# A seven-product (Strassen–Winograd) projection: four output sums made inside PSUM instead of on VectorE

## The chip, the cores and the metric

The kernel runs on 1 core of one Trainium2 chip. The metric is device time in microseconds (us). Three runs of the kernel before gave 979.81, 979.97 and 980.25 us; their median, 979.97 us, is the time to which everything is compared.

## The reference

One layer of an encoder, on x of 512 tokens by 2048 columns, in float32. A combined input projection gives q, k, v and a gate for two groups of 16 heads; group A runs dilated sliding-window attention, group B a two-dimensional neighbourhood attention; the gated outputs go through one output projection and a layer norm.

```python
h = jnp.einsum('bsd,de->bse', x, w_in[layer])
qa, ka, va, ga, qb, kb, vb, gb = jnp.split(h, splits, axis=-1)
ya = _dilated_attention(heads(qa), heads(ka), heads(va), t5_bias)
yb = _neighbourhood_attention(heads(qb), heads(kb), heads(vb), na_rpb[layer])
ya = merge(ya) * jax.nn.silu(ga.astype(jnp.float32))
yb = merge(yb) * jax.nn.silu(gb.astype(jnp.float32))
y = jnp.concatenate([ya, yb], axis=-1).astype(x.dtype)
out = jnp.einsum('bse,ed->bsd', y, w_out[layer])
x = _layer_norm(DEEPNORM_ALPHA * x + out, ln_gain[layer], ln_bias[layer])
```

The change touches only how qa, ka, va, qb, kb and vb are computed, each a product of x (512 by 2048) with a weight block of 2048 by 1024.

## The kernel before, in words

**Precision.** A float32 operand is split into a high part and a low part (`split`, L86): ScalarE (ACT) copies it rounded to the high part, VectorE (DVE) subtracts to get the low part. Each product then takes three matmuls: high by high, high by low, low by high.

**Stages.** From 0 to about 71 us a plain block (L259) loads and splits x and computes six gate columns. From there to about 547 us run six seven-product blocks (`strassen_block`, L341), in the order k, q, v of group A and k, q, v of group B. Then comes attention, mixed with the remaining gate columns and the first half of the output projection as filler matmuls, to about 900 us, and last the rest of the output projection and the norm.

**A seven-product block.** x and the weights are cut into two by two quarters; seven products of sums of quarters replace eight plain ones. The four weight quarters are called q0, q1, q2 and q3, each in four tiles `braw` of 128x1024 (512 KB), loaded by `load` (L345) through SyncE's DMA queue (SP). Quarters are changed in place: `add` (L358) makes q0+=q1, q1+=q3, q0+=q3 and q0+=q2 as the products go on. The products run in the order 1, 5, 7, 6, 3, 2, 4. Each has four steps u (called jobs below, 28 per block); a job is 24 matmuls of 256 columns (k and q) or 12 of 512 columns (v), on two PSUM banks `acc` (t = 0 and 1).

**Who runs ahead.** `run_blocks` (L452) writes the order of TensorE (PE), DVE and ACT by hand. In iteration n DVE adds for job n+3 (`add`), ACT makes the high part of job n+2 (`high`, L362), then come the functions listed in `behind` for iteration n (loads, sums and stores), then DVE makes the low part of job n+2 (`low`, L367), and PE runs job n. So ACT and DVE are some two jobs ahead of PE. The order of SP's queue is not written by hand: the framework's scheduler sets it, and the queue is worked through in that order.

**PSUM.** Eight banks: four in pool `pacc`, two in `pss` (scores use it later) and two in `pst` (transposes use it later). Product 1 takes the two of `pss`, 5 and 7 those of `pacc`, 6 those of `pst`, 3 again `pss`, 2 and 4 again `pacc`.

**Sums.** After product 6, `combine_` (L431) makes on DVE, for each t, w = r1 - p6 (r1 is a copy of p1 made by ACT, L429), u3 = w - p7, c22 = p5 - u3 and w = p5 - w. `plus` (L438) then adds p3 to w, p2 to r1 and p4 to u3. That is 7 operations for each t, 84 over the six blocks. Each result is stored (`store_kq` L229, `store_v` L217): ACT copies it to `kst` or `vst`, DVE subtracts for the low part, SP writes both to `k_d`, `q_d` or `v_d` in DRAM.

**Shared memory slots.** The four sums r1, w, u3, c22 of a block lie in slots t0 to t3. After the last block the attention's first tiles take them over: `load_kq` (L534) puts k of the first pair of heads into t0 and q into t1 (two DMAs of 256 KB, L544), `load_v` (L547) puts its v into t2. `scores(0)` (L607) is the first work of attention that PE does; it stands in PE's order 49 gate matmuls (L516) behind the last block. SP's loads of weights for these, `wraw` (L495), are in the same queue.

**A side job.** In the first block, behind product 5, `rows` (L146) makes two small matmuls L149 for the bias table, on banks of `pss`.

Of the kernel before, what the change touches and what calls it, by code (L numbers as in the profile page):

```python
# [10 lines left out]
ALU = mybir.AluOpType  # L11
# [59 lines left out]
def hybrid_layer(tc, xT, xn, w_in, w_early, w_gate, w_out, t5x, brow, rpb, cmask, eye, gain, lbias, out):  # L71
    nc = tc.nc
    from contextlib import ExitStack
    with ExitStack() as ctx:
# [4 lines left out]
        pacc = ctx.enter_context(tc.tile_pool(name="pacc", bufs=4, space=bass.MemoryType.PSUM))  # L79
        pss = ctx.enter_context(tc.tile_pool(name="pss", bufs=2, space=bass.MemoryType.PSUM))  # L80
        pst = ctx.enter_context(tc.tile_pool(name="pst", bufs=2, space=bass.MemoryType.PSUM))
# [24 lines left out]
        def bank(pool, name):  # L106
            tag = {id(pacc): "acc", id(pss): "sc", id(pst): "pt"}[id(pool)]
            return pool.tile([128, 512], F32, name=name, tag=tag)
# [29 lines left out]
        def prep_a():  # L138
            nc.gpsimd.dma_start(ident, eye)
            bt = ring_b.next("bias")  # L140
            t5 = bt[0:33, 1024:1040]
            nc.gpsimd.dma_start(bt[0:33, :ROW], brow)
            nc.gpsimd.dma_start(t5, t5x)
            row = ring_b.next("bias")

            def rows():  # L146
                for i in range(2):
                    ps = bank(pss, "sc")
                    nc.tensor.matmul(ps[0:16], t5, bt[0:33, 512 * i:512 * i + 512], start=True, stop=True)  # L149
                    nc.scalar.activation(row[0:16, 512 * i:512 * i + 512], ps[0:16], AF.Copy)  # L150
                for c in range(16):
                    nc.gpsimd.dma_start(rows_d[:, c], row[0:16, :ROW])
            return rows
# [94 lines left out]
        def store(kind, g, ch, half, t, src):  # L248
            if kind == "v":
                store_v(g, ch, half, t, src)  # L250
            else:
                store_kq(kind, g, ch, half, t, src)
# [69 lines left out]
        def combine(k, xr, sums):  # L322

            a11, a21, a12, a22 = (xr[:, s, HALF * i:HALF * i + HALF] for s in range(2) for i in range(2))
            c = sums.next("sums")[:, :1024].rearrange("p (n q) -> p n q", n=4)
            nc.vector.tensor_tensor(c[:, 0], a21, a22, ALU.subtract)
            nc.vector.tensor_tensor(c[:, 1], a11, c[:, 0], ALU.subtract)
            nc.vector.tensor_tensor(c[:, 2], a12, c[:, 1], ALU.subtract)
            nc.vector.tensor_tensor(c[:, 3], a21, a11, ALU.subtract)
            split(c[:, 0], A5[k][:, 0], A5[k][:, 1])  # L330
            split(c[:, 1], A6[k][:, 0], A6[k][:, 1])
            split(c[:, 2], A3[k][:, 0], A3[k][:, 1])
            split(c[:, 3], X[k][:, 0, HALF:], X[k][:, 1, HALF:])
# [7 lines left out]
        def strassen_block(src, kind, g, hooks):  # L341

            base = len(jobs)

            def load(q, tags):  # L345
                def run():
                    for u in range(4):
                        raw = slot(tags[u], F32, "braw")
                        nc.sync.dma_start(raw, src[4 * q + u])
                        raws[q].append(raw)  # L350
                return run

            raws = {q: [] for q in range(4)}

            def product(i, pool, q, other=None):
                accs = []

                def add(u):  # L358
                    if other is not None:
                        nc.vector.tensor_tensor(raws[q][u], raws[q][u], raws[other][u], ALU.add)  # L360

                def high(u):  # L362
                    h = halves.next("wh", F32R)
                    nc.scalar.activation(h, raws[q][u], AF.Copy)  # L364
                    return h

                def low(u, h):  # L367
                    l = halves.next("wl", F32R)
                    nc.vector.tensor_tensor(l, raws[q][u], f(h), ALU.subtract)  # L369
                    return h, l  # L370

                def run(u, h, l):
                    if u == 0:
                        accs.extend(bank(pool, "acc") for _ in range(2))
                    for t in range(2):
                        for kk in range(2):
                            k = 2 * u + kk
                            ah, al = operand(i, k)
                            if kind == "k":
                                ah, al = (m.rearrange("p (b r c) -> p r b c", r=4, b=4) for m in (ah, al))  # L380
                            if kind == "v":
                                c = slice(512 * kk, 512 * kk + 512)
                                q = slice(128 * t, 128 * t + 128)
                                nc.tensor.matmul(accs[t], ah[:, q], h[:, c], start=k == 0, stop=False)  # L384
                                nc.tensor.matmul(accs[t], al[:, q], h[:, c], start=False, stop=False)  # L385
                                nc.tensor.matmul(accs[t], ah[:, q], l[:, c], start=False, stop=k == 7)  # L386
                                continue
                            for n in range(2):
                                c = slice(512 * kk + 256 * t + 128 * n, 512 * kk + 256 * t + 128 * n + 128)
                                o = accs[t][:, HALF * n:HALF * n + HALF]  # L390
                                nc.tensor.matmul(o, h[:, c], ah, start=k == 0 and n == 0, stop=False)  # L391
                                nc.tensor.matmul(o, h[:, c], al, start=False, stop=False)  # L392
                                nc.tensor.matmul(o, l[:, c], ah, start=False, stop=k == 7 and n == 1)  # L393
                    if u == 3:
                        next(hooks, lambda: None)()

                jobs.extend((lambda u=u: add(u), lambda u=u: high(u), lambda h, u=u: low(u, h),
                             lambda h, l, u=u: run(u, h, l)) for u in range(4))
                return accs

            def at(product_, u, fn):

                behind.setdefault(base + 4 * product_ + u, []).append(fn)

            def sub(o, x, y):
                nc.vector.tensor_tensor(o, x, y, ALU.subtract)

            made = {}

            def pair(name):  # L410
                if name not in made:
                    t = temps.next(name)
                    made[name] = [t[:, :512], t[:, 512:]]
                return made[name]

            p1 = product(1, pss, 0)
            p5 = product(5, pacc, 0, 1)
            p7 = product(7, pacc, 1, 3)
            p6 = product(6, pst, 0, 3)
            p3 = product(3, pss, 3)  # L420
            p2 = product(2, pacc, 2)
            p4 = product(4, pacc, 0, 2)
            tags = list(sets)
            for q, ahead, i in ((0, 10, 0), (1, 4, 1), (3, 2, 2)):
                behind.setdefault(base - ahead if base else -4, []).append(load(q, tags[i]))
            at(2, 2, load(2, tags[1]))

            def keep(t):
                nc.scalar.activation(pair("r1")[t], p1[t], AF.Copy)  # L429

            def combine_(t):  # L431
                r1, w, u3, c22 = (pair(n)[t] for n in ("r1", "w", "u3", "c22"))
                sub(w, r1, p6[t])
                sub(u3, w, p7[t])
                sub(c22, p5[t], u3)
                sub(w, p5[t], w)

            def plus(name, p, t):  # L438
                o = pair(name)[t]
                nc.vector.tensor_tensor(o, p[t], o, ALU.add)  # L440

            for t in range(2):
                at(1, t, lambda t=t: keep(t))
                at(4, t, lambda t=t: combine_(t))
                for n, name, p in ((5, "w", p3), (6, "r1", p2), (7, "u3", p4)):
                    at(n, t, lambda t=t, name=name, p=p: plus(name, p, t))
            for t in range(2):
                for n, name, ch, half in ((4, "c22", 1, 1), (5, "w", 1, 0), (6, "r1", 0, 0), (7, "u3", 0, 1)):
                    at(n, t + 1, lambda t=t, name=name, ch=ch, half=half: store(kind, g, ch, half, t, pair(name)[t]))
            sets[0], sets[2] = sets[2], sets[0]  # L450

        def run_blocks():  # L452
# [307 lines left out]
        with tc.manual_schedule(engines=engines):  # L760
# [6 lines left out]
            for n in range(136):  # L767
                b, i = n % 4, n // 8
# [177 lines left out]
        for dc in (2, 3):  # L946
            for u in range(4, 8):
                raw = out_ring.next("wraw")
                nc.sync.dma_start(raw[:, :1024], w_out[8 * dc + u])
                i = 2 * (u - 4)  # L950
# [80 lines left out]
```

## Time and profile before

| what | value |
|---|---|
| median of three runs | 979.97 us (979.81 to 980.25) |
| span of the profiled execution | 978.4 us |
| PE, matmul busy | 968.1 us |
| PE, weight loads busy (PEld) | 855.0 us |
| DVE busy | 756.8 us |
| ACT busy | 486.6 us |
| SP's queue, share of 16 DMA engines' span | 56.6% |
| granted TensorE clock, mean | 0.996 |

The profile gives the span of one profiled execution, from its first to its last instruction, and no time of its own beside it; the median of the runs is 1.57 us above that span. A matmul's row gives its start and its modelled length; since matmuls are pipelined, the pace of PE is read from the distance of the starts. A row of the DMA-issuing queue (SPq) tells when a transfer was issued, not when it landed.

### The profile page before, as it was taken

How to read it: one execution, taken by the hardware profiler on the slowest of the kernel's cores; microseconds unless marked ns; L12 is line 12 of the kernel's file. 1: busy time of each engine (PE TensorE's matmuls, PEld its weight loads, DVE VectorE, ACT ScalarE, POOL GpSimd, SP SyncE). 2: the span in 40 equal slices, each digit the busy share in tenths (PEclk: the TensorE clock that was granted, in tenths of full speed). 3: DMA queues.
4: the chain of work that ended last, by engine and by line, in shares of the span. 5: the costliest groups of instructions: out<-in, count | busy, mean ns of one | idle time of the engine just before them, and what ended most of it. 6: DMA issues, size and time to landing. Idle time of an engine off the chain costs nothing.

```text
span 978.4 us, 16019 instructions
## 1 busy us (share of the span) xinstructions
PE 968.1 (99%) x5851; PEld 855.0 (87%) x5851; DVE 756.8 (77%) x1152; ACT 486.6 (50%) x839; POOL 179.0 (18%) x327
## 2 busy tenths in 40 slices
PE   9999999999999999999999999999999999999996
PEld 6889999999888999999888888888888888888885
DVE  7947788788988977878889567676676767777877
ACT  7534344344444434434454366666666666762300
POOL 1000665664553400000000001010010000100021
PEclk9999999999999999999999999999999999999998
DMA  9731688599569638428634967777777788768322
GB/s 341 289 120 55 164 276 270 177 255 273 178 188 302 185 95 277 116 87 232 165 120 113 343 185 217 194 232 234 188 222 224 197 238 205 209 223 293 90 75 97
DMA packets 118014, 194.29 MB, mean 199 GB/s; under 512 B 48351, under 2 KB 67551, under 8 KB 117936
## 3 DMA queue, kind: packets, MB, share of 16 engines
q1 hardware_dynamic: 105104, 169.15, 56.6%
q0 software_dynamic: 12256, 23.47, 8.7%
q8 instruction: 46, 0.75, 0.3%
q10 hardware_dynamic: 576, 0.66, 0.2%
q14 instruction: 32, 0.26, 0.1%
HBM read 148.68 MB, written 44.50 MB: 197 GB/s over the span
## 4 chain that ended last, share of the span: by engine, by line
PE 96%; DVE 1%; ACT 1%; DMA 1%; issue 0%; SPq 0%; DVEq 0%; ACTq 0%
PE acc L710 15%; PE acc L516 11%; PE acc L391 11%; PE acc L393 11%; PE acc L392 11%; PE acc L384 5%; PE acc L386 5%; PE acc L385 5%; PE pv L662 4%; PE pt L640 4%; PE acc L270 2%; PE sc L621 2%; PE acc L272 2%; PE acc L271 2%; PE sc L620 2%; PE sc L710 1%
## 5 line engine op out<-in xcount | busy, mean ns | idle before, releaser
L364 ACT ACTIVATE wh<-braw 128x1024 fp32r<-128x1024 f32 x168 | 178.3, 1061 | 254.9 <-PE acc L392 130.9
L369 DVE TENSOR_TENSOR wl<-braw,wh 128x1024 fp32r<-128x1024 f32 x168 | 206.4, 1229 | 65.6 <-ACT wh L364 65.3
L391 PE MATMUL acc<-xk,wh 128*128 128x256 f32 x512 | 144.5, 282 | 0.0
L393 PE MATMUL acc<-xk,wl 128*128 128x256 f32 x512 | 144.4, 282 | 0.0
L392 PE MATMUL acc<-xk,wh 128*128 128x256 f32 x512 | 144.4, 282 | 0.0
L360 DVE TENSOR_TENSOR braw<-braw 128x1024 f32<-128x1024 f32 x96 | 118.8, 1237 | 0.0
L710 PE MATMUL acc<-wh,yk 128*128 128x512 f32 x320 | 108.4, 402 | 0.0
L392 PE MATMUL acc<-op,wh 128*128 128x256 f32 x384 | 108.4, 282 | 0.0
L391 PE MATMUL acc<-op,wh 128*128 128x256 f32 x384 | 108.3, 282 | 0.0
L393 PE MATMUL acc<-op,wl 128*128 128x256 f32 x384 | 108.3, 282 | 0.0
L646 DVE TENSOR_TENSOR tl<-pt,th 128x256 fp32r<-128x256 f32 (+1 forms) x128 | 71.1, 555 | 48.0 <-ACT th L645 46.8
L391 PEld LDWEIGHTS acc<-xk,wh 128*128 128x128 f32 x512 | 97.2, 190 | 0.9 <-ACT bias L150 0.9
L392 PEld LDWEIGHTS acc<-xk,wh 128*128 128x128 f32 x512 | 97.2, 190 | 0.1
L393 PEld LDWEIGHTS acc<-xk,wl 128*128 128x128 f32 x512 | 97.2, 190 | 0.0
L645 ACT ACTIVATE th<-pt 128x256 fp32r<-128x256 f32 (+1 forms) x128 | 62.3, 489 | 65.0 <-PE pt L640 62.9
L516 PE MATMUL acc<-xk,wh 128*128 128x512 f32 x320 | 90.8, 402 | 0.0
L577 DVE CUSTOM_DVE_ANT_0 s<-sc,biases 128x512 f32<-128x512 f32 (+2 forms) x128 | 68.1, 532 | 17.9 <-PE sc L621 17.3
L581 ACT ACTIVATE p<-s,mn 128x512 f32<-128x512 f32 (+1 forms) x96 | 62.1, 647 | 25.6 <-DVE mn L577 25.2
L392 PEld LDWEIGHTS acc<-op,wh 128*128 128x128 f32 x384 | 72.9, 190 | 0.0
L393 PEld LDWEIGHTS acc<-op,wl 128*128 128x128 f32 x384 | 72.9, 190 | 0.0
L391 PEld LDWEIGHTS acc<-op,wh 128*128 128x128 f32 x384 | 72.9, 190 | 0.0
L710 PEld LDWEIGHTS acc<-wh,yk 128*128 128x128 f32 x320 | 58.4, 189 | 9.1 <-ACT yk L694 0.3
(183 smaller groups left out, 2026.1 us busy)
## 6 DMA issues: line engine op xcount, KB each, us to landing
braw<-in_w_in SPq DMA_DIRECT2D x96, 512.0 KB
wraw<-in_w_out SPq DMA_DIRECT2D x32, 512.0 KB
wraw<-in_w_gate SPq DMA_DIRECT2D x20, 512.0 KB
k_d<-kst SPq DMA_DIRECT2D x64, 128.0 KB
q_d<-kst SPq DMA_DIRECT2D x64, 128.0 KB
v_d<-vst SPq DMA_DIRECT2D x32, 256.0 KB
q<-q_d SPq DMA_DIRECT2D x32, 256.0 KB
k<-k_d SPq DMA_DIRECT2D x16, 512.0 KB
```

Source lines behind the costliest of these rows:

```text
L360: nc.vector.tensor_tensor(raws[q][u], raws[q][u], raws[other][u], ALU.add)
L364: nc.scalar.activation(h, raws[q][u], AF.Copy)
L369: nc.vector.tensor_tensor(l, raws[q][u], f(h), ALU.subtract)
L391: nc.tensor.matmul(o, h[:, c], ah, start=k == 0 and n == 0, stop=False)
L392: nc.tensor.matmul(o, h[:, c], al, start=False, stop=False)
L393: nc.tensor.matmul(o, l[:, c], ah, start=False, stop=k == 7 and n == 1)
L516: nc.tensor.matmul(acc, w[:, k * 128:k * 128 + 128], X[8 * u + k][:, s], start=u == 0 and n == 0 and k == 0, stop=u == 1 and n == 2 and k ...
L577: nc.vector.tensor_tensor_reduce(*flat, bias, 1.0, 3e38, ALU.add, ALU.min, mn)
L581: nc.scalar.activation(p[:, to:to + n].rearrange("p (b r c) -> p b r c", r=8, c=c), s[:, :n].rearrange(order, r=8, c=c), AF.Exp, bias=mn, ...
L645: nc.scalar.activation(th, pt[:, :nch], AF.Copy)
L646: nc.vector.tensor_tensor(tl, pt[:, :nch], f(th), ALU.subtract)
L710: nc.tensor.matmul(acc[:, part], yk[k][:, s, c], w[:, wk], start=first and kk == 0 and n == 0, stop=last and kk == 1 and n == 2)
```

## The change

Products 2, 3 and 4 no longer get banks of their own. Product 2 runs on top of product 1's banks, product 3 on product 5's and product 4 on product 7's: their matmuls have no start flag, so that PSUM adds them to what is there. For that, the order of the last three products becomes 2, 3, 4, and the operand of product 7 changes its sign (a11 - a21 instead of a21 - a11).

The sums become: w = r1 - p6; u3 = p7 + w; c22 = p5 - u3 (before products 2, 3 and 4 write on the banks); then c11 is product 1's bank itself, from which ACT and DVE store directly; c12 = p5 - w goes to r1; c21 = p7 + w goes to w. That is 5 operations for each t, 60 over six blocks. c11, c12 and c21 are stored in this order, in the iterations in which w, r1 and u3 were. In the last block, w (slot t1) is thus read last by c21, and u3 (slot t2) is done with after `combine_`.

The load of the next block's q0, into the slots that q3 leaves, is listed six iterations ahead of that block instead of ten, since q3 is used one product later. The load of q2 stays in iteration 10 of its block, and q2 is used one product earlier. The two small matmuls L149 get banks of `pst`, since those of `pss` are held longer.

```diff
             def rows():
                 for i in range(2):
-                    ps = bank(pss, "sc")
+                    ps = bank(pst, "pt")
...
-            nc.vector.tensor_tensor(c[:, 3], a21, a11, ALU.subtract)
+            nc.vector.tensor_tensor(c[:, 3], a11, a21, ALU.subtract)
...
-            def product(i, pool, q, other=None):
-                accs = []
+            def product(i, pool, q, other=None, onto=None):
+                accs = [] if onto is None else onto
+                first, skip = onto is None, onto is not None
...
-                    if u == 0:
+                    if u == 0 and first:
                         accs.extend(bank(pool, "acc") for _ in range(2))
...
-                                nc.tensor.matmul(o, h[:, c], ah, start=k == 0 and n == 0, stop=False)
+                                nc.tensor.matmul(o, h[:, c], ah, start=first and k == 0 and n == 0, stop=False, skip_group_check=skip)
...
-            p3 = product(3, pss, 3)
-            p2 = product(2, pacc, 2)
-            p4 = product(4, pacc, 0, 2)
+            product(2, None, 2, onto=p1)
+            product(3, None, 3, onto=p5)
+            product(4, None, 0, 2, onto=p7)
             tags = list(sets)
-            for q, ahead, i in ((0, 10, 0), (1, 4, 1), (3, 2, 2)):
+            for q, ahead, i in ((0, 6, 0), (1, 4, 1), (3, 2, 2)):
...
                 sub(w, r1, p6[t])
-                sub(u3, w, p7[t])
+                nc.vector.tensor_tensor(u3, p7[t], w, ALU.add)
                 sub(c22, p5[t], u3)
-                sub(w, p5[t], w)
-
-            def plus(name, p, t):
-                o = pair(name)[t]
-                nc.vector.tensor_tensor(o, p[t], o, ALU.add)
+
+            def last(name, t):
+                r1, w = pair("r1")[t], pair("w")[t]
+                if name == "c12":
+                    sub(r1, p5[t], w)
+                    return r1
+                if name == "c21":
+                    nc.vector.tensor_tensor(w, p7[t], w, ALU.add)
+                    return w
+                return p1[t] if name == "c11" else pair("c22")[t]
...
-                for n, name, p in ((5, "w", p3), (6, "r1", p2), (7, "u3", p4)):
-                    at(n, t, lambda t=t, name=name, p=p: plus(name, p, t))
             for t in range(2):
-                for n, name, ch, half in ((4, "c22", 1, 1), (5, "w", 1, 0), (6, "r1", 0, 0), (7, "u3", 0, 1)):
-                    at(n, t + 1, lambda t=t, name=name, ch=ch, half=half: store(kind, g, ch, half, t, pair(name)[t]))
+                for n, name, ch, half in ((4, "c22", 1, 1), (5, "c11", 0, 0), (6, "c12", 1, 0), (7, "c21", 0, 1)):
+                    at(n, t + 1, lambda t=t, name=name, ch=ch, half=half: store(kind, g, ch, half, t, last(name, t)))
```

**What moves, place 1: SP's queue at the end of the first block.** `braw` are the weight tiles, `k_d<-kst` the stores of this block's results (eight DMAs for c22, then four for each half of the next). Before:

```order
L319 DMA sg_d<-sg 128x512 x6
L349 DMA braw<-in_w_in 128x1024 x7
L243 DMA k_d<-kst 64x2x256 x8
L349 DMA braw<-in_w_in 128x1024 x2
L243 DMA k_d<-kst 64x2x256 x4
```

Now:

```order
L319 DMA sg_d<-sg 128x512 x6
L349 DMA braw<-in_w_in 128x1024 x4
L243 DMA k_d<-kst 64x2x256 x8
L349 DMA braw<-in_w_in 128x1024 x4
L243 DMA k_d<-kst 64x2x256 x4
```

The seven loads ahead of c22's stores were four of q2 and three of the next block's q0; now only q2's four stand there, and all four of the next q0 stand behind the stores.

**Place 2: DVE at the end of the last block.** `r` and `u` are r1 and u3, `wl<-wraw` is the low part of a gate weight of the next stage, `vst` the low part of a stored result. Before:

```order
L223 TENSOR_TENSOR vst<-r_5368,vst 128x8x64
L502 TENSOR_TENSOR wl<-wraw,wh 128x1024 x2
L440 TENSOR_TENSOR u_5586<-acc,u_5586 128x512 x2
L502 TENSOR_TENSOR wl<-wraw,wh 128x1024
L223 TENSOR_TENSOR vst<-u_5586,vst 128x8x64 x2
```

Now:

```order
L223 TENSOR_TENSOR vst<-r_5318,vst 128x8x64
L506 TENSOR_TENSOR wl<-wraw,wh 128x1024
L444 TENSOR_TENSOR w<-acc,w 128x512
L223 TENSOR_TENSOR vst<-w,vst 128x8x64
L444 TENSOR_TENSOR w<-acc,w 128x512
L506 TENSOR_TENSOR wl<-wraw,wh 128x1024
L223 TENSOR_TENSOR vst<-w,vst 128x8x64
```

The last two sums stood together and their low parts behind the third gate weight; now sum and low part alternate, and the last reader of w (slot t1) is the last of them.

**Place 3: SP's queue at the turn to attention.** `q<-q_d` x2 is the load of q for the first pair, without which `scores(0)` can't start; `v_d<-vst` are the stores of the last block. Before:

```order
L544 DMA q<-q_d 64x2x512 x2
L495 DMA wraw<-in_w_gate 128x1024 x4
L226 DMA v_d<-vst 64x4x256 x4
L542 DMA k<-k_d 128x1024
L495 DMA wraw<-in_w_gate 128x1024 x3
L604 DMA biases<-biasa_d 128x560
L226 DMA v_d<-vst 64x4x256 x4
L553 DMA vv<-v_d 128x1024
```

Now:

```order
L499 DMA wraw<-in_w_gate 128x1024
L226 DMA v_d<-vst 64x4x256 x2
L546 DMA k<-k_d 128x1024
L499 DMA wraw<-in_w_gate 128x1024
L226 DMA v_d<-vst 64x4x256 x2
L499 DMA wraw<-in_w_gate 128x1024
L608 DMA biases<-biasa_d 128x560
L226 DMA v_d<-vst 64x4x256 x2
L548 DMA q<-q_d 64x2x512 x2
```

The load of q for the first pair has gone from ahead of four gate weights to behind the last store of v; the load of `vv` has gone the other way, ahead of all stores of v.

More of the change, by code (lines that the diff above doesn't have):

```diff
@@ L383, in run @@
                                 q = slice(128 * t, 128 * t + 128)
-                                nc.tensor.matmul(accs[t], ah[:, q], h[:, c], start=k == 0, stop=False)
-                                nc.tensor.matmul(accs[t], al[:, q], h[:, c], start=False, stop=False)
-                                nc.tensor.matmul(accs[t], ah[:, q], l[:, c], start=False, stop=k == 7)
+                                nc.tensor.matmul(accs[t], ah[:, q], h[:, c], start=first and k == 0, stop=False, skip_group_check=skip)
+                                nc.tensor.matmul(accs[t], al[:, q], h[:, c], start=False, stop=False, skip_group_check=skip)
+                                nc.tensor.matmul(accs[t], ah[:, q], l[:, c], start=False, stop=k == 7, skip_group_check=skip)
                                 continue
@@ L390, in run @@
                                 o = accs[t][:, HALF * n:HALF * n + HALF]
-                                nc.tensor.matmul(o, h[:, c], ah, start=k == 0 and n == 0, stop=False)
-                                nc.tensor.matmul(o, h[:, c], al, start=False, stop=False)
-                                nc.tensor.matmul(o, l[:, c], ah, start=False, stop=k == 7 and n == 1)
+                                nc.tensor.matmul(o, h[:, c], ah, start=first and k == 0 and n == 0, stop=False, skip_group_check=skip)
+                                nc.tensor.matmul(o, h[:, c], al, start=False, stop=False, skip_group_check=skip)
+                                nc.tensor.matmul(o, l[:, c], ah, start=False, stop=k == 7 and n == 1, skip_group_check=skip)
                     if u == 3:
```

## The prediction

> **What bounds the kernel now.** I read the page first, then what PE waited for, then the stage of the six seven-product blocks alone.
>
> ```profile
> span 978.4 us, 16019 instructions
> PE 968.1 (99%) x5851; PEld 855.0 (87%) x5851; DVE 756.8 (77%) x1152; ACT 486.6 (50%) x839; POOL 179.0 (18%) x327
> PE 96%; DVE 1%; ACT 1%; DMA 1%; issue 0%; SPq 0%; DVEq 0%; ACTq 0%
> ```
>
> PE is busy for 99% of the span, and the chain of work that ended last runs through PE for 96% of it. The list of waits of PE and of its weight loads (engine and line, who ended the wait, total, times, longest):
>
> ```profile
> PE pt L909 <- DVE nms L907: 2.5, 1, 2.5
> PE sc L124 <- POOL calm L121: 1.3, 1, 1.3
> PEld acc L391 <- ACT bias L150: 0.9, 1, 0.9
> ```
>
> The two longest lie at the start (L124) and in the last norm (L909). In the six blocks there is one, 0.9 us, behind the bias table's matmuls. The stage by itself (PE, PEld, DVE, ACT, POOL busy, then clock, DMA share, GB/s):
>
> ```profile
> 92.00:540.00 448.00, 448.00 (x3161) 421.29 (x3160) 373.28 (x381) 199.98 (x224) 135.02 (x253) 1.00 0.65 193
> ```
>
> PE has no gap in 448 us, at the full granted clock; DVE is at 373.28 of 448, that is 83%, and is not waited for. So whatever the change takes from DVE here is taken from an engine that has time left, and the time moves only if PE's own work, its pace, or a wait of PE changes.
>
> **The sums.** Per block and half, 7 operations become 5, so 24 of 84 go.
>
> ```profile
> L440 DVE TENSOR_TENSOR w<-acc,w 128x512 f32<-128x512 f32 x12 | 8.2, 684 | 0.0
> L440 DVE TENSOR_TENSOR r<-acc,r 128x512 f32<-128x512 f32 x12 | 8.2, 684 | 0.0
> ```
>
> 24 operations of 684 ns are 16.4 us of DVE. They lie beside PE's work, which the list of waits shows not to wait for DVE there: worth 0. On the other side the change removes no matmul and adds none: 3360 in the six blocks before and now. That products 2 to 4 add onto a bank instead of starting one is what all but the first matmul of a product do already, at the same pace: 0. Their banks must have been read first (p1 by ACT's copy, p5 and p7 by `combine_`); those reads stand a product or more earlier in the order, 11 us at least, so no wait. The stores of c11 read PSUM instead of SBUF, on two engines with time to spare: 0. The sign of the operand: 0. The bias matmuls on banks of `pst`: these are free until product 6, one product later: 0.
>
> **The weight loads.** q2 is issued as before and used one product, four jobs, earlier; q0 of the next block is issued four jobs later, behind c22's stores (place 1). Is there room? SP's queue at the end of the first block, and ACT's first uses of the next block's q0:
>
> ```profile
> 115.50 6.87 SPq L349 DMA_DIRECT2D braw<-in_w_in  x3
> 125.29 5.31 SPq L243 DMA_DIRECT2D k_d<-kst  x8
> 130.64 3.27 SPq L349 DMA_DIRECT2D braw<-in_w_in  x2
> 147.03 1.06 ACT L364 ACTIVATE wh<-braw 128x1024 fp32r<-128x1024 f32 x1 [1.25 <-PE acc L392]
> 155.55 1.06 ACT L364 ACTIVATE wh<-braw 128x1024 fp32r<-128x1024 f32 x1 [1.81 <-DMA k_d<-kst]
> ```
>
> The first of them was issued at 115.50 and used at 147.03. Now all four start behind the stores, from about 130.6 us on, and are used at 147.03 to 155.55: the margin of the first shrinks from 31 to 16 us. For q2 the first load was issued at 90.78 (in the fence below) and now is wanted by ACT about two jobs ahead of product 2's place, 118.6 - 5.8 = 112.8 us with a product of 11.3 us: 22 us of room. What a load takes under full load is shown at the turn to attention:
>
> ```profile
> 90.78 31.59 SPq L349 DMA_DIRECT2D braw<-in_w_in  x7
> 534.29 1.78 SPq L544 DMA_DIRECT2D q<-q_d  x2
> 536.16 2.21 SPq L495 DMA_DIRECT2D wraw<-in_w_gate  x4
> 541.99 1.06 ACT L501 ACTIVATE wh<-wraw 128x1024 fp32r<-128x1024 f32 x1 [1.20 <-DMA wraw<-in_w_gate]
> 545.00:557.00 12.00, 12.00 (x54) 9.95 (x53) 4.93 (x6) 2.29 (x4) 0.00 (x0) 1.00 1.03 362
> ```
>
> ACT waited until 541.99 for a tile of the same 512 KB whose issue began at 536.16: 5.8 us from issue to use. 5.8 is well below 16 and 22, so the loads stay hidden: 0. That ACT waits for a `braw` load hardly at all now agrees (3.7 us in two waits for a load, against 187.8 us for PE to free a buffer):
>
> ```profile
>   PE acc L392: 130.9, 78
>   PE acc L385: 56.9, 37
>   DMA braw<-in_w_in: 3.7, 2
> ```
>
> **The one load that comes too late.** Slot t1 holds w. Before, w's last reader stood in the last product but one, and q of the first pair was issued at 534.29, long before `scores(0)` needs it. Now w is read last by c21 at the very end (place 2), and q stands behind the last store of v (place 3). What ends the block, and when PE wants q:
>
> ```profile
> 546.36 1.35 DVE L440 TENSOR_TENSOR u<-acc,u 128x512 f32<-128x512 f32 x2
> 547.81 1.13 ACT L222 ACTIVATE vst<-u 128x512 fp32r<-128x512 f32 x2
> 547.93 1.23 DVE L502 TENSOR_TENSOR wl<-wraw,wh 128x1024 fp32r<-128x1024 f32 x1 [0.22 <-ACT wh L501]
> 549.08 1.29 DVE L223 TENSOR_TENSOR vst<-u,vst 128x512 fp32r<-128x512 f32 x2
> 550.25 3.83 SPq L226 DMA_DIRECT2D v_d<-vst  x4
> 557.70 0.19 PEld L620 LDWEIGHTS sc<-k,q 128*128 128x128 f32 x1
> bias<-rows_d POOLq DMA_DIRECT2D x128, 35.0 KB, 3.4
> sg_d<-sgo POOLq DMA_DIRECT2D x10, 256.0 KB, 4.7
> ```
>
> By the new order DVE goes on from 546.36 with: sum 0.68, ACT's copy 0.6, low part 0.69, sum 0.68, third gate weight 1.23, low part 0.69, which ends at 550.9, about 551.0 with the handovers (before: 549.08 + 1.29 = 550.4). Then SP issues two stores, at 3.83 / 4 = 0.97 us each (0.6 where it isn't held up), and q's two DMAs, of which the second begins 1.78 / 2 = 0.89 us behind the first: 551.0 + 1.9 + 0.9 = 553.8 at the latest, 552.9 at 0.6 each. Take 553.6. From issue to landing I have three rows: 3.4 us for a 35 KB DMA of POOL, 4.7 us for POOL's 256 KB, the same size, and the 5.8 us above for 512 KB on this queue. The DMA engines are full here (share 1.03 from 545 to 557), which speaks against the low end. Landing: 552.9 + 3.4 = 556.3, 553.6 + 4.7 = 558.3, or 553.8 + 5.8 = 559.6. PE's weight load for `scores(0)` began at 557.70, and every matmul of PE queues behind it. So PE stands for 0, 0.6 or 1.9 us. I take 0.6, from the row of the same size, and keep 0 and 1.9; that PE doesn't stand at all has a quarter of the chance. In the stages behind it PE has no gap in which this would be given back.
>
> Here a rule can be weighed. The Trainium skill, "DMA: Bandwidth & Descriptors", Anatomy of one DMA, gives a fixed cost of about 2.0 us plus the bytes at 436 GB/s; by it 256 KB would take an estimated 2.6 us, q would land at about 556.2 and PE would not stand at all, which makes the sum 0.6 us smaller. The trace disagrees for this stage, with 4.7 us for the same size.
>
> **PE's pace.** The starts of k's matmuls show two paces in one block. Rows of PE, the first and last of 88 and of 59 matmuls, and the bias matmuls between the two stretches:
>
> ```profile
> 83.51 0.28 PE L393 MATMUL acc<-op,wl 128*128 128x256 f32 x1
> 93.95 0.28 PE L393 MATMUL acc<-op,wl 128*128 128x256 f32 x1
> 94.16 1.89 PE L149 MATMUL sc<-bias 33*16 33x512 f32 x4
> 139.49 0.28 PE L391 MATMUL acc<-xk,wh 128*128 128x256 f32 x1
> 146.31 0.28 PE L392 MATMUL acc<-xk,wh 128*128 128x256 f32 x1
> ```
>
> Before the bias matmuls 10.44 us / 87 = 120.0 ns from start to start; after them 6.82 / 58 = 117.6 ns, to the end of that block. A product of 96 such matmuls gains 0.23 us by the second pace, the five products left in this block 1.2 us. I don't know what sets it; it begins right behind L149. L149 stays where it is, so I keep the pace: 0. If the new bank upsets it, 1.2 us are lost; if other blocks of k or q should fall into it, each gains up to 7 x 0.23 = 1.6 us, all 23 products now at 120 ns 5.3 us.
>
> **The sum.** Of the profiled execution: 978.4 + 0.6 = 979.0; the 1.57 us by which the median lies above this span I leave as they are. So 979.97 + 0.6 = 980.6 us.
>
> **Rivals.**
> The weights come late (slower). Place 1 puts q0 behind the stores; the next q1 and q3 follow in the same queue, so some 1.5 MB move into the stretch that is fullest. If the first tile took over 16 us from issue to use, ACT's `high` and with it PE would wait, once at each of five turns of blocks: each 1 us beyond that point costs 5 us, 985 us for the first. For it: the queue is worked through in order, and at the turn to attention the DMA share is 1.03. Against: 5.8 us measured there. Chance 0.10.
> q comes later still (slower). If q's two DMAs wait behind all of the gate weights and stores, with 8 us instead of 5.8 from issue to landing, PE stands until 561.8, over 4 us: 984. The point from which it leaves "no change" is a landing at 559.7. Chance 0.10.
> PE is not full (faster). The 968.1 us busy are of modelled ends. In the row of the stage the weight loads take 421.29 of 448.00 us, 94%; if the 26.7 us left were a slackness that DVE's work causes, less DVE would free some of it, or of the pace: with all of k and q at 117.6 ns, 980.6 - 5.3 = 975.3 us. The Trainium skill, "Perfetto Trace Analysis", Identifying the Most-Contended Engine, says just that matmul busy time is no good measure of headroom and that weight-load time is. Against it here: the starts are 120.0 ns apart over 88 matmuls without one irregular step, and the waits name no DVE in this stage. Chance 0.08.
> That the change doesn't do what it says can be left out: DVE's order has 24 rows fewer.
>
> **The numbers.** No change is my forecast, 0.72. Two kernels this close can be told apart by about 0.2%, which is 1.96 us: faster means below 978.0, slower above 981.9. Faster 0.08, same 0.72, slower 0.20. The range takes in both ends of q's landing and the loss of the faster pace upward, 979.9 + 1.9 + 1.2 = 983.0, and a gain of one k or q block's pace without any wait for q downward, 980.6 - 1.6 = 979.0.
>
> **What would show it.** Right: DVE busy lower by about 16 us and the span within 2 us; in the list of waits one new row, PE or PEld at `sc<-k,q`, released by the DMA of q, of 0 to 2 us at about 558 us; no `braw` among the waits of PE. Wrong: ACT idle before its high parts for `braw` by many us at each block's start; a wait of PE for q of 3 us or more; or starts of k's and q's matmuls closer than 120 ns in blocks where they are not now.

## The result: 985.74 us, slower by half a per cent

| | before | changed |
|---|---|---|
| median of four runs | 979.89 us (979.39 to 980.25) | 985.74 us (982.07 to 986.57) |
| ratio, with 95% interval | | 1.0053 [1.0041, 1.0064] |
| profiled execution, time | | 986.57 us |
| its span | 978.4 us | 984.8 us |
| granted TensorE clock, mean | 0.996 | 0.992 |

The kernel before has one run more here than in its table above, so its median is 979.89 and not 979.97 us. The changed kernel is slower by 5.9 us. The forecast was 980.6 us in a range up to 983.0, so it was wrong: the wait that it named came, at the place that it named, but several times as long, and something came behind it that no step had foreseen.

The page of the changed kernel (span; busy time of each engine; the granted clock in 40 slices; the shares of the chain that ended last):

```profile
span 984.8 us, 15984 instructions
PE 971.0 (99%) x5851; PEld 857.8 (87%) x5851; DVE 742.0 (75%) x1128; ACT 487.7 (50%) x839; POOL 180.3 (18%) x327
PEclk9999999999999999999999899999999999999998
PE 95%; DVE 1%; ACT 1%; DMA 1%; issue 0%; SPq 0%; POOL 0%; DVEq 0%; ACTq 0%; POOLq 0%
```

DVE is down from 756.8 to 742.0 us with 24 instructions fewer, as meant, and nothing of that reached the span. One digit is new: slice 23 of 40, about 542 to 566 us, has a clock below 9. The stage of the six blocks by itself, in the same columns as before (PE, PEld, DVE, ACT, POOL, clock, DMA share, GB/s):

```profile
92.00:540.00 448.00, 448.00 (x3161) 421.31 (x3161) 357.92 (x356) 200.81 (x224) 136.23 (x253) 1.00 0.64 195
```

PE had no gap there before and has none now; 15.4 us of DVE are gone and PE's row is the same, 448.00 us and 3161 matmuls. So the loss lies behind the blocks. The list of waits shows where:

```profile
PEld sc L624 <- issue: 4.3, 1, 4.3
PE sc L624 <- DMA q<-q_d: 4.0, 1, 4.0
PEld acc L392 <- ACT bias L150: 0.9, 1, 0.9
```

The last row is the old one. The first two are one and the same new wait, seen from the weight load and from the matmul: `scores(0)` stood for q. No row of PE or PEld names a `braw`. The timeline of DVE at that place (start, duration, operation, and in brackets what was waited for), and that of SP's queue:

```profile
547.29 0.69 DVE L444 TENSOR_TENSOR w<-acc,w 128x512 f32<-128x512 f32 x1 [0.81 <-PE acc L387]
549.29 0.69 DVE L444 TENSOR_TENSOR w<-acc,w 128x512 f32<-128x512 f32 x1
551.02 0.68 DVE L223 TENSOR_TENSOR vst<-w,vst 128x512 fp32r<-128x512 f32 x1
```

```profile
552.00 0.64 SPq L608 DMA_DIRECT2D biases<-biasa_d  x1
552.74 1.24 SPq L226 DMA_DIRECT2D v_d<-vst  x2
554.03 2.10 SPq L548 DMA_DIRECT2D q<-q_d  x2
```

The first sum starts at 547.29 where the forecast had 546.36, the last low part ends at 551.70, SP is then busy with `biases` until 552.64, issues the two stores and comes to q at 554.03. What happened to q stands in the chain of waits that ended last (start, duration, what):

```profile
554.88 7.07 DMA q<-q_d
561.94 0.14 issue
562.08 0.77 PE sc L624
```

7.07 us from the second issue to the landing. And then PE, first before, then changed:

```profile
557.70 0.39 PE L516 MATMUL acc<-xk,wh 128*128 128x512 f32 x1
557.93 0.39 PE L620 MATMUL sc<-k,q 128*128 128x512 f32 x1
558.38 2.43 PE L516 MATMUL acc<-xk,wh 128*128 128x512 f32 x10
```

```profile
557.74 0.39 PE L520 MATMUL acc<-xk,wh 128*128 128x512 f32 x1
562.08 0.77 PE L624 MATMUL sc<-k,q 128*128 128x512 f32 x1 [3.95 <-DMA q<-q_d]
563.07 4.27 PE L520 MATMUL acc<-xk,wh 128*128 128x512 f32 x10
```

PE reached the same point at the same time, 557.7. `scores(0)` then starts 562.08 - 557.93 = 4.15 us late. But the span is 6.4 us longer. The last rows tell where the other 2.2 us went: the same ten matmuls take 4.27 us instead of 2.43. The windows of the changed kernel (columns as above, the clock third from the end):

```profile
555.00:560.00 5.00, 3.13 (x14) 2.25 (x12) 0.00 (x0) 0.60 (x1) 0.00 (x0) 1.00 1.04 320
560.00:562.00 2.00, 0.00 (x0) 0.00 (x0) 0.00 (x0) 0.00 (x0) 0.00 (x0) 0.54 1.01 250
562.00:564.00 2.00, 1.92 (x5) 1.56 (x6) 0.69 (x3) 0.00 (x0) 0.00 (x0) 0.50 1.04 213
564.00:566.00 2.00, 2.00 (x6) 1.58 (x5) 0.61 (x3) 1.76 (x3) 0.59 (x1) 0.50 0.40 101
566.00:568.00 2.00, 2.00 (x8) 1.57 (x7) 0.16 (x1) 0.00 (x0) 0.00 (x0) 0.76 0.34 131
568.00:570.00 2.00, 2.00 (x11) 1.58 (x10) 1.68 (x3) 0.82 (x2) 0.00 (x0) 1.00 0.00 0
```

The granted clock falls to a half while PE stands (0.54 in 560 to 562 is a half from about 560.2 on) and comes back at about 567.0 (0.76 in 566 to 568). From 562.1 to 567.0 PE works at half speed: 4.9 us in which 2.4 us of work are lost. 4.15 + 2.4 = 6.55 us, and the span is 6.4 us longer: the two terms are the loss, to 0.2 us.

### The profile page after: what moved, and what is told of

It is laid out like the page before. It is cut to its first block, busy times and chain, and to the rows that moved or that the text cites. A ratio compares the mean times of both kernels' runs of the same rounds, so it can differ in the third digit from the quotient of the medians.

```text
span 984.8 us, 15984 instructions
## 1 busy us (share of the span) xinstructions
PE 971.0 (99%) x5851; PEld 857.8 (87%) x5851; DVE 742.0 (75%) x1128; ACT 487.7 (50%) x839; POOL 180.3 (18%) x327
## 4 chain that ended last, share of the span: by engine, by line
PE 95%; DVE 1%; ACT 1%; DMA 1%; issue 0%; SPq 0%; POOL 0%; DVEq 0%; ACTq 0%; POOLq 0%
PE acc L714 14%; PE acc L392 11%; PE acc L394 11%; PE acc L393 11%; PE acc L520 10%; PE acc L386 5%; PE acc L387 5%; PE acc L385 5%; PE pv L666 4%; PE pt L644 4%; PE acc L270 2%; PE acc L271 2%; PE acc L272 2%; PE sc L625 2%; PE sc L624 2%; PE sc L714 1%
## 5 line engine op out<-in xcount | busy, mean ns | idle before, releaser
L392 PEld LDWEIGHTS acc<-xk,wh 128*128 128x128 f32 x512 | 97.2, 190 | 0.9 <-ACT bias L150 0.9
L393 PEld LDWEIGHTS acc<-xk,wh 128*128 128x128 f32 x512 | 97.2, 190 | 0.1
L520 PE MATMUL acc<-xk,wh 128*128 128x512 f32 x320 | 92.8, 409 | 0.0
L520 PEld LDWEIGHTS acc<-xk,wh 128*128 128x128 f32 x320 | 58.4, 193 | 10.1
```

Source lines behind the costliest of these rows:

```text
L392: nc.tensor.matmul(o, h[:, c], ah, start=first and k == 0 and n == 0, stop=False, skip_group_check=skip)
L393: nc.tensor.matmul(o, h[:, c], al, start=False, stop=False, skip_group_check=skip)
L520: nc.tensor.matmul(acc, w[:, k * 128:k * 128 + 128], X[8 * u + k][:, s], start=u == 0 and n == 0 and k == 0, stop=u == 1 and n == 2 and k ...
```

## The experiments

The theory to be tried: the whole loss comes from one line, the one that gives the last sum of the block to slot t1, in which q is to land; first as a stand of PE, then as a half clock that the stand brings. The rivals: the rest of the change costs something of its own, as sums that read PSUM longer, a change of PE's order or pace, or a DMA queue with more in it; or the saving on DVE is worth something that is hidden behind the loss.

Times of a run are given beside runs of the kernel before on the same chip; those had medians of 979.75 us (first four), 979.73 (e5) and 979.87 us (e6, e7).

**e1_after_swap: the changed kernel with the late sum in another slot.** u3 and w change their slots, so that the sum that is read last lies in t2, which v takes over much later, and t1 is done with after `combine_`.

```diff
-                r1, w, u3, c22 = (pair(n)[t] for n in ("r1", "w", "u3", "c22"))
+                r1, u3, w, c22 = (pair(n)[t] for n in ("r1", "u3", "w", "c22"))
```

> The changed kernel with w and u3 changing slots: u3, done with after the seven products' first sums, lies in t1, which q of the first pair takes over; w lies in t2. Nothing else differs. Theory T (all of the loss is q's late load at the turn to attention: 4.0 us that PE stands and then half the TensorE clock for 6.8 us): q is issued before the stores of v again, PE has no wait at sc<-k,q, time 979.9 us, at most 0.6 us off; DVE's 16 us less are worth nothing. Rival P (adding onto banks in PSUM, or the later weight loads, cost time in the six blocks): about 985.7 us, as the changed kernel. Rival D (lighter DVE is worth something that the loss hid): below 979.0 us.

Measured: 979.5 us (978.18 to 981.78, 11 runs), ratio 0.9999 [0.9991, 1.0008]. Its page, its timeline of SP's queue and its timeline of PE:

```profile
PE 967.2 (99%) x5851; PEld 854.8 (87%) x5851; DVE 743.1 (76%) x1128; ACT 487.7 (50%) x839; POOL 181.1 (19%) x327
```

```profile
518.01 0.63 SPq L548 DMA_DIRECT2D q<-q_d  x1
520.35 0.59 SPq L548 DMA_DIRECT2D q<-q_d  x1
```

```profile
556.93 0.39 PE L624 MATMUL sc<-k,q 128*128 128x512 f32 x1
```

q is issued some 35 us earlier, `scores(0)` has no wait, and the loss is gone. All else of the change is still there, the 24 sums fewer among it: DVE has 743.1 us. So the rest of the change costs nothing that can be measured, and it also brings nothing: 13.7 us of DVE work taken away are worth 0 here, within 0.1%, which is 0.9 us either way. Both kinds of rival fall, as far as they were to explain 5.9 us.

**e2_before_swap: the same edit in the kernel before.** None of the change's work, only the late slot.

```diff
-                r1, w, u3, c22 = (pair(n)[t] for n in ("r1", "w", "u3", "c22"))
+                r1, u3, w, c22 = (pair(n)[t] for n in ("r1", "u3", "w", "c22"))
```

> The kernel before with the same two slots exchanged, so that u3, read last at the very end of the last block, lies in t1 and q of the first pair must wait for it. Seven sums, own banks for all products. Theory T: the loss appears without any of the change's work: PE stands 3 to 5 us at sc<-k,q, granted clock halved behind it, 984 to 987 us. Rival P: no more than 980.5 us.

Measured: 982.6 us (982.58 to 984.72, 5 runs), ratio 1.0036 [1.0024, 1.0049]: slower, but by less than was expected. Its list of waits and its chain:

```profile
PEld sc L620 <- issue: 2.6, 1, 2.6
PE sc L620 <- DMA q<-q_d: 2.2, 1, 2.2
```

```profile
555.20 5.28 DMA q<-q_d
560.61 0.47 PE sc L620
```

A loss of this kind, about half as large, appears without any of the change. In the profiled execution it is the stand alone, 2.6 us, and the span grows by 2.4 us, from 978.4 to 980.8; the half clock that was expected behind it is missing there, and the mean clock stayed 0.996. q lands 5.28 us after its second issue here, 7.07 in the changed kernel.

**e3_after_busy: the changed kernel, PE kept at work while q is on its way.** 16 matmuls that nobody uses, on one bank, ahead of `scores(0)`; 16 at 0.227 us are 3.6 us.

```diff
+                if n == 0:
+                    spare = bank(pacc, "acc")
+                    for _ in range(16):
+                        nc.tensor.matmul(spare, X[0][:, 0, 0:128], X[0][:, 0], start=True, stop=True)
```

> The changed kernel with 16 matmuls of 512 columns, whose result nobody reads, ahead of scores(0): 16 x 0.227 = 3.6 us of work in the time in which PE stood. Theory T with the clock as a term of its own: PE stands only some 0.5 us, the granted clock stays at 1.0, and the time is that of before plus 4.1 = 984.0 us (983.4 to 984.6), with little spread between runs. If the halved clock costs nothing: as the changed kernel, 985.7 to 986.5 us. If PE's stand were hidden work that could be filled at a cost: 985.7 + 3.6 = 989.3 us.

Measured: 983.5 us (982.39 to 984.26, 5 runs), ratio 1.0038 [1.0026, 1.0051]. PE at that place, and the clock:

```profile
556.65 3.79 PE L787 MATMUL acc<-xk 128*128 128x512 f32 x16
560.41 0.47 PE L624 MATMUL sc<-k,q 128*128 128x512 f32 x1
560.96 2.43 PE L520 MATMUL acc<-xk,wh 128*128 128x512 f32 x10
```

```profile
560.00:562.00 2.00, 2.00 (x9) 1.40 (x9) 0.84 (x3) 0.11 (x1) 0.00 (x0) 1.00 1.05 229
```

The ten matmuls behind take 2.43 us again, at a clock of 1.00. q is issued as late as before: at 552.94, in a profiled execution in which PE gets to this place 1.1 us earlier. Useless work in place of the stand makes the kernel faster by 985.74 - 983.5 = 2.2 us. So the half clock is a term of its own. Of the 2.2 us some 0.5 are only that 3.6 us of useless work are less than a stand of 4.15, which leaves 1.7 us for the clock; the trace gave 2.4. The runs of the changed kernel scatter by more than this difference, so about 2 us is all that can be said of its size. The rest, 983.5 - 979.75 = 3.75 us, is the 3.6 us of useless work, to 0.15 us.

**e4_after_mid: the changed kernel, c21 written into u3's slot.** Another way to the same end as e1: w's last reader is then the sum itself, and not the store's two steps behind it.

```diff
-                    nc.vector.tensor_tensor(w, p7[t], w, ALU.add)
-                    return w
+                    u3 = pair("u3")[t]
+                    nc.vector.tensor_tensor(u3, p7[t], w, ALU.add)
+                    return u3
```

> The changed kernel with c21 written into u3's slot instead of w's: w (t1) is then free behind the last sum, some 1.7 us earlier on DVE, and SP's order has q ahead of the last two stores of v, the last gate weight and the biases. Theory T: q is issued at about 550 to 552 us instead of 554 to 555, PE stands 0 to 1.5 us, too short for the clock to fall: 979.9 to 981.4 us. Rival P: 985.7 us.

Measured: 979.76 us (977.94 to 980.82, 11 runs), ratio 0.9998 [0.9989, 1.0007]. q's two issues moved from 554.0 to 550.6 (the timelines of SP's queue and of PE):

```profile
550.61 1.86 SPq L549 DMA_DIRECT2D q<-q_d  x2
```

```profile
557.83 0.39 PE L625 MATMUL sc<-k,q 128*128 128x512 f32 x1
```

No wait is left. With e1, e4 and the changed kernel there are three times of q's first issue, 518.0, 550.6 and 554.0, and the loss sets in between the last two; in e7, below, an issue at 552.9 still costs 2.2 us.

**e7_q_pool: the changed kernel, q issued by POOL.** What the 7.07 us consist of was still open: q's place behind other transfers in SP's queue, or engines that are full whoever issues. Only the first pair's q is moved to the other queue.

```diff
-                nc.sync.dma_start(f(to), q_d[g][j][n // 2].rearrange("(a c) q -> c a q", a=2))
+                (nc.sync if i or n > 1 else nc.gpsimd).dma_start(f(to), q_d[g][j][n // 2].rearrange("(a c) q -> c a q", a=2))
```

> The changed kernel, with the two DMAs of the first pair's q issued by POOL instead of SP. Slot t1 is free at 551.7 us, so POOL can issue them at about 551.8 and 552.5 us, without the two stores of v ahead of them (SP issued them at 554.0 and 554.9). Theory A: the 7.0 us from the second issue to the landing were time behind SP's own queue. Then they land as POOL's 256 KB did elsewhere, 4.7 us behind the second issue, at about 557.2 us, when PE reaches scores(0) at 558.1: no wait, no half clock, 979.5 to 980.5 us. Theory B: they were the 16 DMA engines, full whatever queue is used. Then the landing is again about 7 us behind the second issue, at 559.5, and PE stands some 1.5 us, too short for the clock to halve: 981 to 982 us. In both the loss falls below half of the 5.9 us; if it stays above 4 us, the lateness of the slot is not what costs.

Measured: 982.09 us (980.38 to 983.08, 11 runs), ratio 1.0019 [1.0011, 1.0028]. Its chain of waits and its list of waits:

```profile
552.94 0.62 POOL q L548
553.56 7.29 DMA q<-q_d
561.10 0.47 PE sc L624
```

```profile
PEld sc L624 <- issue: 2.5, 1, 2.5
PE sc L624 <- DMA q<-q_d: 2.1, 1, 2.1
```

Theory B holds: on POOL's queue, where nothing else had been issued in the ten us before, q takes 7.29 us. So it is not SP's queue; what is left is that the 16 engines are full, with a DMA share of 0.87 from 554 to 556 us and of 0.98 to 1.07 from there to 562. The Trainium skill, "DMA: Bandwidth & Descriptors", Issuing engines are not separate DMA queues, says just this, that DMAs of all issuing engines end on the same 16 DMA engines and interleave there; these two numbers, 7.07 and 7.29 us, agree. The smaller loss comes from the earlier issue, without the stores ahead, and from a stand of 2.1 us behind which the clock stayed at 1.00 in the profiled execution. The issue was later than expected, 552.94 for about 551.8: all of this execution runs 0.8 us later, and the chain has the load of the first pair's k, which landed at 552.68, just ahead of it.

**e5_pace: e1 with small matmuls that might set PE's pace.** The prediction had left open why k's matmuls run at 117.6 ns behind the bias matmuls L149 and at 120.0 ns elsewhere. Two fp32 matmuls with weights of 33x16, like those (a pair shows as four records), ahead of the first product of blocks 1 (q, 512 columns), 3 (k, 512 columns) and 4 (q, 64 columns), counted from 0.

```diff
+                    if u == 0 and i == 1 and base in (28, 84, 112):
+                        w_ = 64 if base == 112 else 512
+                        for _ in range(2):
+                            spare = bank(pst, "pt")
+                            nc.tensor.matmul(spare[0:16, 0:w_], f(X[0][0:33, 0, 0:16]), f(X[0][0:33, 0, 0:w_]), start=True, stop=True)
```

> The changed kernel with the slots exchanged, plus two float32 matmuls of 33 rows and 16 columns of weights, like the bias table's L149, whose result nobody reads, ahead of product 1 of the second block (q, 512 columns moved), the fourth (k, 512) and the fifth (q, 64). Question: is it such a matmul that brings k's matmuls from 120.0 to 117.6 ns from start to start? If it is, the k block behind it runs at 117.6 ns (1.6 us less over seven products), the two q blocks too if it isn't tied to k's access pattern, and the time is 979.5 + 3 x 1.9 at most for the added work - 1.6 to 4.8 us. If it is not: all three blocks at 120.0 ns, time 979.5 plus about 4.2 us for the added matmuls.

Measured: 982.85 us (982.57 to 983.1, 6 runs), ratio 1.0033 [1.002, 1.0046]. The matmuls cost about 2 us for each pair of 512 columns (1.89 us in the row at the end of this text), more than the pace gives back. The pace itself is read from how many matmuls start in 50 us of a block; first k of group B (320 to 370), then q (400 to 450), in the changed kernel and in e5:

```profile
320.00:370.00 50.00, 50.00 (x419) 50.00 (x418) 39.52 (x38) 20.03 (x21) 5.85 (x13) 1.00 0.36 101
400.00:450.00 50.00, 50.00 (x419) 50.00 (x418) 38.96 (x38) 20.15 (x22) 0.00 (x0) 1.00 0.35 94
```

```profile
320.00:370.00 50.00, 50.00 (x428) 50.00 (x427) 40.41 (x39) 20.92 (x23) 6.22 (x13) 1.00 0.37 101
400.00:450.00 50.00, 50.00 (x419) 50.00 (x419) 39.44 (x39) 20.61 (x22) 0.00 (x0) 1.00 0.32 88
```

428 for 419, by 2%, which is 120.0 / 117.6, in the block of k; q stays at 419. So the faster pace follows such a matmul, and in k alone. That the matmul itself is what sets it is not shown: it also breaks PE's even row of matmuls, and in the profiled execution of e1, which has no such matmul in this block, the same block goes over to the faster pace behind two waits of PE of 0.2 us.

**e6_best: e1 with the cheapest of these.** Two matmuls of 64 columns, ahead of block 3 alone; the edit is shown against e5.

```diff
-                    if u == 0 and i == 1 and base in (28, 84, 112):
-                        w_ = 64 if base == 112 else 512
+                    if u == 0 and i == 1 and base == 84:
+                        w_ = 64
```

> The changed kernel with u3 and w having changed their slots (979.5 us), and two 64-column fp32 matmuls with 33x16 weights ahead of product 1 of the fourth block (k of group B), on banks of pst. By the run with such matmuls ahead of three blocks they cost about 0.5 us and set the faster pace of 117.6 ns in a block of k for all of its seven products, 7 x 0.23 = 1.6 us: 978.4 us, or no gain beside 979.5 us in those executions in which this block falls into the faster pace by itself. If the pace needs the longer, 512-column matmuls, 980.0 us.

Measured: 978.65 us (978.29 to 980.73, 11 runs), ratio 0.9991 [0.9982, 1.0]. Its page and the block of k:

```profile
span 976.6 us, 15994 instructions
```

```profile
320.00:370.00 50.00, 50.00 (x427) 50.00 (x426) 39.86 (x38) 21.19 (x23) 5.67 (x13) 1.00 0.39 110
```

The pace is the faster one. This is the lowest median of all kernels here, 7 us below the changed kernel and 1.2 us below the kernel before; but the interval reaches to 1.0 and overlaps with e1's, so that it beats the kernel before, or e1, is likely and not settled.

## Why the prediction was wrong

**What bounds the kernel: right.** PE without a gap in the blocks, DVE's relief worth 0. e1 shows it directly, with all of the relief and the old time. The one exception is small: in the profiled executions of e1 and e3, PE waited for DVE's low part twice, 0.4 us in all, in the fourth block.

**The sums, the adding onto banks, the reads of PSUM, the sign, the bias matmuls: right.** All at 0, within 0.1%; e1 holds them all and runs at 0.9999 of the time before. DVE fell by 14.8 us where 16.4 had been worked out; where the 1.6 us are was not looked into, since none of it lies on PE's path.

**The weight loads: right.** No wait of PE names one. ACT waited 2.9 us for `braw` in two waits, 3.7 before. The first rival falls.

**q: the right wait, the wrong size.** The wait of 3 us or more that was to show it wrong is there. The step that failed is the size of PE's stand, "Take 553.6" and "I take 0.6, from the row of the same size, and keep 0 and 1.9", with nothing added for what comes behind a stand. Term by term:

- The issue. Worked out was an end of the low part at 551.0 and the second issue at 553.6, at the latest 553.8. Measured: 551.70 and 554.88. 0.7 us come from PE's order, which the prediction did not read at this place; it read DVE's and SP's. The block no longer ends in one piece: seven gate matmuls (L520) now stand ahead of its last ten and 42 behind them, where before all 49 stood behind. The weight loads of the seven take 1.55 us,

```profile
544.37 1.55 PEld L520 LDWEIGHTS acc<-xk,wh 128*128 128x128 f32 x7
```

  so the last product ends later, and its sums with it, while PE as a whole loses nothing. Another 1.0 us passes from 551.70 to 552.74, in which SP is held by the issue of `biases`; the two stores then took 0.62 us each and not 0.97, which gives 0.65 us back. Against the 553.6 taken, it is 1.3 us later in all.
- The landing. 4.7 us was taken, with 5.8 as the upper end; measured were 7.07, 5.28 (e2) and 7.29 us (e7). The row of the same size was POOL's: the median of ten stores to DRAM, which took 3.0 to 6.6 us and were issued between 560.3 and 726.4 us, behind the stretch in question and not in it, where the prediction's "for this stage" puts it. The size was the same and the stretch was not: here the DMA share is 1.03 to 1.04. The prediction saw that number and used it only against the low end. The Trainium skill, "DMA: Bandwidth & Descriptors", Anatomy of one DMA, gives its fit for DMAs that GpSimd (POOL) issues, and q was issued by SP; by it the transfer would be an estimated 2.6 us. The trace disagrees with that still more clearly than with the 4.7, in e7 too, where POOL issues.
- The sum of both, 1.3 + 2.4 = 3.7 us, is the stand: 0.6 + 3.7 = 4.3, as the list of waits has it.
- The half clock. Not in the prediction at all: about 2 us, 2.4 by the trace and 1.7 by e3. A bound that stops at the length of the wait is too low once the clock falls behind it. The profile of the kernel before could have told: behind the 2.5 us wait in the last norm (L909), which the prediction lists, the granted clock is 0.50.

The rival "q comes later still" had landing times and a price of this kind, 984 us, and a chance of 0.10. It was the case that came true, with a landing at 561.9 where it had 561.8, but by a path of later issue and full engines and not by the one it named, the queue: e7 took q out of that queue, and the landing took as long. With some 2 us for the clock its 984 would have been 986.

**The pace: kept.** In the profiled execution the blocks of the changed kernel run at the paces of before; the third rival, PE not full, falls with e1.

What stays open: the loads and stores whose bytes fill the engines between 545 and 562 us were not taken apart, so why 5.28 us in e2 and 7.07 in the changed kernel is not settled.

## What to carry to other kernels

When an edit makes a buffer's last reader later, look for the next owner of that buffer, and cost its transfer at the length that transfers have in that very stretch, with the DMA share beside it; a row of the same size from a quieter place is no price. Where a wait falls on an engine that had none, ask whether it is long enough to change the clock, and add that price. And read the order of every engine at the place: here the engine that "changes nothing" moved the end of a product by more than a microsecond.

## What the runs showed of the hardware

- A stand of PE of 4.0 us brought a half clock of about 6.8 us (560.2 to 567.0); stands of 2.2 us (e2) and 2.1 us (e7) did not, in their profiled executions. The wait of 2.5 us in the last norm of the kernel before did: PE's last matmul ahead of it ends at 968.5, the clock falls at about 970.6 and is 0.50 from 971 on. So the stands that brought the half clock, 2.5 and 4.0 us, and those that did not, 2.1 and 2.2 us, lie close together. The Trainium skill, "TensorE: Matmul & The Clock Gate", Part 1, tells of a free-running window of about 3.4 us, of which an idle one halves the clock. Two such windows would be an estimated 6.8 us, and the trace agrees; but the clock fell some 2 us after PE's last matmul (558.1), earlier than a whole window, and the trace decides. By a free-running window the same stand may be caught or not, and the runs look like that: in the four runs of the changed kernel the fastest, 982.07 us, has a mean clock of 0.995 and the others, 985.34 to 986.57 us, 0.992 to 0.994. e2's runs divide in the same way, three at 982.58 to 982.6 us with 0.996 and two at 983.49 and 984.72 us with 0.994; e7's do so less clearly. These other runs have no profile, so this is a reading and not shown.
- Behind an fp32 matmul with small weights, the 256-column matmuls of k ran at the faster of two paces, 117.6 for 120.0 ns, to the end of the block; those of q did not. The pair costs little if it is short: e6's is

```profile
309.02 0.39 PE L380 MATMUL pt<-xk 33*16 33x64 f32 x4
```

  and e5's, with 512 columns,

```profile
311.14 1.89 PE L380 MATMUL pt<-xk 33*16 33x512 f32 x4
```

  In the profiled executions of e1 and e3, block 3 took the faster pace without such a matmul, in its second product (product 5), behind two waits of about 0.2 us for DVE's low part. So the break in PE's row of matmuls may be what counts and not the matmul; in e4 two breaks of less than 0.1 us at the same place left the pace at 120.0 ns. What sets the pace, and why in k and not in q, is open; that its being taken or not makes part of the scatter of 978.2 to 981.8 us in e1's runs is a guess from this one case.
